# One store for the last group's output, and larger, earlier loads in the first third, in a tree-masked attention kernel

## The chip, the core and the metric

The kernel runs on one core of one Trainium2 chip. The time is the device time of one execution in microseconds, the median of several runs. A profile is one execution taken by the hardware profiler; its span is the time from the first instruction to the last, and the profiled execution's own time is a little longer than its span.

## The reference

Eight batches of twelve heads make 96 heads. Each has 512 queries and keys of 64 numbers. The mask lets a query see itself and its ancestors in a binary heap:

```python
mask = np.zeros((seq, seq))
for i in range(seq):
    mask[i, i] = 1
    parent = i
    while parent > 0:
        parent = (parent - 1) // 2
        mask[i, parent] = 1
scores = np.einsum('bhqd,bhkd->bhqk', Q, K) / np.sqrt(dim) + (1 - mask) * (-1e9)
weights = np.exp(scores - scores.max(-1, keepdims=True))
weights = weights / (weights.sum(-1, keepdims=True) + 1e-10)
return np.einsum('bhqk,bhkd->bhqd', weights, V).astype(np.float32)
```

Q, K, V and the output are each 96 x 512 x 64 floats, 12.58 MB.

## The kernel before, in words

The work is cut into 48 pairs of heads (loop index `i`) and into 12 groups of eight heads, or four pairs, each (index `g`). "q24" below means the load of Q for the heads from 24 on; v, k and q name V, K and Q.

**Loads.** `load_v`, `load_k` and `load_q` (line 189) issue one DMA each from GpSimd's queue. The DMA casts from float32 in DRAM to bf16 in SBUF, so an eight-head load reads 1 MB and writes 512 KB; a four-head load is half of that. There are four buffers of eight heads for each of V, K and Q. Which loads are issued after which pair is a table written out by hand, `loads_at` (line 447): the dictionary `early` up to pair 12, and one load per pair from a formula after that.

**One pair.** TensorE transposes K and Q of the pair into PSUM (line 250), VectorE copies them out (line 276), TensorE makes scores for two key tiles (lines 287 to 316), ScalarE takes the exponentials (lines 298 and 321), TensorE multiplies by V (line 347), and VectorE normalises (reciprocal, line 376, and multiply, line 377) into an output tile `of` of the group. Transposes run two pairs ahead: in turn `i` of the main loop (line 497) the order is scores of pair `i`, values and normalisation of pair `i-1`, transposes and copy of pair `i+2`, then `spread(i)` and `pool(i)`.

**Spreading V.** The values of a group have to be copied into a second layout `vt` (line 209). `spread(i)` (line 425) divides these copies among VectorE, GpSimd and, early on, ScalarE. From pair 6 on the first of GpSimd's copies in a turn waits for the VectorE copy of the same turn (`after`, line 390), so that the two alternate. These are GpSimd's "waiting copies".

**GpSimd's queue.** It holds, in program order, the spread copies of a turn and after them, from `pool(i)` (line 473), the loads and the stores of the turn. An instruction that waits holds everything behind it. The DMAs that it issues use eight completion semaphores in turn, so each DMA also waits for the landing of the one eight before it.

**Stores.** `store` (line 384) writes output heads to DRAM, from GpSimd's queue as well; an eight-head store is 1 MB, since the output is float32. `pool(i)` begins to store at pair 33, one group per turn, and takes any group that is complete. After turn 46 the first four heads of group 11, the last, are stored on their own (line 511). In turn 48 the loop in `pool` reaches group 11 too and stores all eight heads. After the loop, heads 4 and 5 and heads 6 and 7 of the group are stored once more (lines 512 and 513). Each of these stores writes DRAM rows that an earlier one wrote, or overlaps it, and the program makes it wait for the landing of that earlier store.

Of the kernel before, what the change touches and what calls it, by code (L numbers as in the profile page):

```python
# [98 lines left out]
def kernel(  # L99
# [15 lines left out]
    NG = NH // GB  # L115
# [68 lines left out]
    def load(kept, pool, name, src, h0, n):  # L184

        g = h0 // GB
        if g not in kept:
            kept[g] = pool.tile([P, GB, 4, D], bf16, name=name)
        nc.gpsimd.dma_start(  # L189
            out=kept[g][:, h0 % GB:h0 % GB + n, :, :].rearrange("p h t d -> p h (t d)"),  # L190
            in_=src[:, h0:h0 + n, :],
        )
# [191 lines left out]
    def store(g, h0=0, n=GB):  # L384
        nc.gpsimd.dma_start(  # L385
            out=Or[:, GB * g + h0:GB * g + h0 + n, :],
            in_=ofs[g][:, h0:h0 + n, :, :].rearrange("p h t d -> p h (t d)"),
        )
# [58 lines left out]
    def loads_at(i):  # L447

        k4 = lambda h: [(load_k, h, 4), (load_q, h, 4)]
        start = [(load_v, 0, 4), (load_k, 2, 2), (load_q, 2, 2)] + k4(4) + [(load_v, 4, 4)]  # L450
        start += k4(8) + [(load_v, 8, 4)] + k4(12)
        early = {
            -1: start, 1: [(load_v, 12, 4), (load_v, 16)],
            2: [(load_k, 16, 4), (load_q, 16, 4), (load_k, 20, 4)],
            3: [(load_q, 20, 4), (load_v, 24), (load_k, 24, 4)], 5: [(load_q, 24, 4)],
            6: [(load_k, 28, 4)], 7: [(load_q, 28, 4), (load_v, 32)],
            8: [(load_k, 32), (load_q, 32)], 9: [(load_v, 40)], 10: [(load_k, 40)],
            11: [(load_q, 40), (load_v, 48)], 12: [(load_k, 48), (load_q, 48)],
        }
        if i in early:  # L460
            return early[i]
        g, j = i // 4 + 3, i % 4
        if i < 13:
            return []
        if j == 0:
            return [(load_q, GB * g)] if g < NG else []
        if j < 3 and g + 1 < NG:
            return [((load_v, load_k)[j - 1], GB * (g + 1))]
        return []

    stored = []

    def pool(i):
        for f, *args in loads_at(i):
            f(*args)
        if i >= 33:
            for g in range(len(stored), (i - 4) // 4 + 1):
                if len(stored) < i - 32:
                    stored.append(g)
                    store(g)  # L480

    AHEAD = {1: (2, 3), 2: (), 3: (4, 5)}

    pool(-1)
    fill(0, 8)
    first_pair()
# [10 lines left out]
    for i in range(1, NP + 1):  # L497
        if i < NP:
            scores1(i)
            scores2(i)  # L500
        if i >= 2:
            values(i - 1)
            norm(i - 1, ((0, 1), (1, 2)) if i == NP else ((0, 2),))
        for n in AHEAD.get(i, (i + 2,)):
            if n < NP:
                transpose(n)
                evac(n)
        spread(i)
        pool(i)
        if i == NP - 2:  # L510
            store(NG - 1, 0, 4)
# [32 lines left out]
```

## Time and profile before

| what | us |
|---|---|
| median of 3 runs | 148.3 (147.78 to 149.77) |
| the profiled execution's own time | 149.07 |
| its span | 147.3 |
| last normalisation starts (VectorE, line 377) | 130.27, 0.42 long |
| last store issued (GpSimd, line 385) | 143.3 |

| engine | busy us | share of the span |
|---|---|---|
| TensorE, matmuls | 114.8 | 78% |
| VectorE | 103.0 | 70% |
| GpSimd | 96.2 | 65% |
| ScalarE | 92.6 | 63% |

DMA is not in this table. Its share and its rate stand in the page's part 2, in 40 slices of the span, 3.68 us each. The rate counts the bytes written: while loads run it is about 198 GB/s, with twice as many bytes read, and while stores run about 400 GB/s. A timeline line gives the start, the length, the engine, the source line, the operation, the tiles, and in brackets how long the engine idled before it and what ended that. The DMA view gives, for the issues in a stretch of time, the time from issue to landing. The chain is followed back from the last instruction to what released it.

### The profile page before, as it was taken

How to read it: one execution, taken by the hardware profiler on the slowest of the kernel's cores; microseconds unless marked ns; L12 is line 12 of the kernel's file. 1: busy time of each engine (PE TensorE's matmuls, PEld its weight loads, DVE VectorE, ACT ScalarE, POOL GpSimd, SP SyncE). 2: the span in 40 equal slices, each digit the busy share in tenths (PEclk: the TensorE clock that was granted, in tenths of full speed). 3: DMA queues.
4: the chain of work that ended last, by engine and by line, in shares of the span. 5: the costliest groups of instructions: out<-in, count | busy, mean ns of one | idle time of the engine just before them, and what ended most of it. 6: DMA issues, size and time to landing. Idle time of an engine off the chain costs nothing. (4 is left out here: it accounts for less than half of the span.)

```text
span 147.3 us, 5481 instructions
## 1 busy us (share of the span) xinstructions
PE 114.8 (78%) x2413; PEld 80.7 (55%) x2413; DVE 103.0 (70%) x215; ACT 92.6 (63%) x110; POOL 96.2 (65%) x134
## 2 busy tenths in 40 slices
PE   6787769998989599999997998998979889910000
PEld 2345547666767377777675775765757566610000
DVE  2586767897999559999796988889887795530000
ACT  4187927999888357887775776777748585800000
POOL 7965996059879974869967588589786873200221
PEclk9999968999999869999999999999999999995555
DMA  4999999998799999999999999999999999995243
GB/s 125 223 194 199 193 197 197 197 188 106 98 191 198 199 197 199 197 198 202 194 199 197 198 201 194 199 197 206 341 399 402 404 397 405 399 394 215 110 176 142
DMA packets 41418, 33.39 MB, mean 227 GB/s; under 512 B 1034, under 2 KB 38026, under 8 KB 41394
## 3 DMA queue, kind: packets, MB, share of 16 engines
q0 software_dynamic: 40656, 32.25, 117.7%
q1 hardware_dynamic: 466, 0.53, 1.1%
q8 instruction: 19, 0.31, 0.8%
q10 hardware_dynamic: 272, 0.26, 0.6%
q14 instruction: 5, 0.04, 0.1%
HBM read 38.01 MB, written 13.63 MB: 351 GB/s over the span
## 5 line engine op out<-in xcount | busy, mean ns | idle before, releaser
L298 ACT ACTIVATE e<-s 128x1024 bf16<-128x1024 f32 x48 | 49.1, 1023 | 32.5 <-PE s L292 32.1
L209 POOL COPY vt<-vst 32x512 bf16<-32x512 bf16 (+2 forms) x69 | 46.5, 674 | 28.6 <-DVE vt L209 22.7
L347 PE MATMUL ob<-vt,e 128*128 128x65 bf16 (+1 forms) x940 | 38.4, 198 | 2.2 <-DVE of L377 0.7
L321 ACT ACTIVATE e<-s 128x768 bf16<-128x768 f32 x48 | 38.7, 806 | 0.3 <-PE s L316 0.3
L347 PEld LDWEIGHTS <-e 128*128 128x128 bf16 (+1 forms) x960 | 31.0, 103 | 10.4 <-issue 2.1
L276 DVE COPY kq<-kqp 128x1024 bf16<-128x1024 bf16 x48 | 32.8, 683 | 5.3 <-PE kqp L250 5.1
L377 DVE TENSOR_TENSOR of<-ob,rec 128x512 f32<-128x512 f32 x47 | 32.5, 692 | 1.6
L209 DVE COPY vt<-vst 32x1024 bf16<-32x1024 bf16 (+2 forms) x60 | 28.4, 473 | 1.6
L385 POOL DMA_DIRECT2D out_dram<-of x15 | 12.8, 857 | 18.1 <-issue 9.4
L250 PE MATMUL kqp<-ptile,kst 128*64 128x128 bf16 x384 | 20.0, 225 | 4.2 <-DVE kq L276 2.0
L250 PE MATMUL kqp<-ptile,qst 128*64 128x128 bf16 x384 | 19.9, 225 | 2.8 <-DMA qst<-in_Q_dram 1.8
L287 PE MATMUL s<-ctile 40*128 40x512 bf16 x96 | 19.2, 395 | 1.2 <-ACT e L298 1.0
L316 PEld LDWEIGHTS <-kq 64*128 64x128 bf16 x384 | 14.7, 95 | 9.5 <-issue 2.4
L292 PE MATMUL s<-kq 64*128 64x512 bf16 x96 | 18.9, 388 | 1.2 <-issue 0.7
L376 DVE RECIPROCAL rec<-ob 128x8 f32<-128x8 f32 x47 | 9.7, 207 | 14.4 <-PE ob L347 12.6
L316 PE MATMUL s<-kq 64*128 64x64 bf16 (+1 forms) x384 | 18.2, 211 | 1.2 <-issue 1.2
L310 PE MATMUL s<-ctile 40*128 40x480 bf16 x96 | 18.0, 370 | 0.5
L250 PEld LDWEIGHTS <-kst 128*64 128x64 bf16 x384 | 13.5, 113 | 5.9 <-issue 5.0
L250 PEld LDWEIGHTS <-qst 128*64 128x64 bf16 x384 | 14.4, 114 | 3.1 <-DMA qst<-in_Q_dram 2.0
L189 POOL DMA_DIRECT2D kst<-in_K_dram x16 | 13.3, 834 | 0.0
L189 POOL DMA_DIRECT2D qst<-in_Q_dram x16 | 13.3, 832 | 0.0
L189 POOL DMA_DIRECT2D vst<-in_V_dram x14 | 12.2, 874 | 0.9 <-POOLq L528 0.8
(22 smaller groups left out, 38.5 us busy)
## 6 DMA issues: line engine op xcount, KB each, us to landing
out_dram<-of POOLq DMA_DIRECT2D x12, 1024.0 KB, 13.0
vst<-in_V_dram POOLq DMA_DIRECT2D x10, 512.0 KB, 13.5
kst<-in_K_dram POOLq DMA_DIRECT2D x8, 512.0 KB, 14.7
qst<-in_Q_dram POOLq DMA_DIRECT2D x8, 512.0 KB, 13.5
kst<-in_K_dram POOLq DMA_DIRECT2D x7, 256.0 KB, 9.7
qst<-in_Q_dram POOLq DMA_DIRECT2D x7, 256.0 KB, 10.2
vst<-in_V_dram POOLq DMA_DIRECT2D x4, 256.0 KB, 7.4
out_dram<-of POOLq DMA_DIRECT2D x1, 512.0 KB, 9.6
```

The source lines that it names most:

```text
L189: nc.gpsimd.dma_start(out=kept[g][:, h0 % GB:h0 % GB + n, :, :].rearrange("p h t d -> p h (t d)"), in_=src[:, h0:h0 + n, :],)
L209: return (eng.copy if eng is nc.scalar else eng.tensor_copy)(out=out, in_=in_)
L250: nc.tensor.transpose(out=dst, in_=st[2 * i // GB][:, 2 * i % GB + a, t, :], identity=perm)
L276: nc.vector.tensor_copy(out=kq[:, :, :, :].rearrange("p k (x y) c -> p k x y c", y=2), in_=src)
L287: nc.tensor.matmul(out=sp[:, a, :], lhsT=k1code[64 * a:64 * a + BITS, :], rhs=q1code[64 * a:64 * a + BITS, :], start=True, stop=False,)
L292: nc.tensor.matmul(out=sp[:, a, :], lhsT=keys(i, a, TOP), rhs=qTs[i][64 * a:64 * a + 64, :, :].rearrange("p t c -> p (t c)"), start=False, ...
L298: nc.scalar.activation(out=et[:, :, :, :].rearrange("p a t c -> p (a t c)"), in_=sp[:, :, :].rearrange("p a c -> p (a c)"), func=AF.Exp, s ...
L310: nc.tensor.matmul(out=flat[:, a, 32:512], lhsT=k2code[64 * a:64 * a + BITS, :], rhs=q2code[64 * a:64 * a + BITS, 32:512], start=True, sto ...
L316: nc.tensor.matmul(out=flat[:, a, lo:hi], lhsT=keys(i, a, TILE2[t]), rhs=qTs[i][64 * a:64 * a + 64, :, :].rearrange("p t c -> p (t c)")[:, ...
L321: nc.scalar.activation(out=e2s[i % NE][:, :, :, 32:128].rearrange("p a t c -> p (a t) c"), in_=sp[:, :, :, 32:128].rearrange("p a t c -> p ...
L347: nc.tensor.matmul(out=ob[lo:hi, a, 65 * t:65 * t + 65], lhsT=e[:, a, PLACE[t], lo:hi], rhs=vt[:, 2 * i % GB + a, tile_v, 0:D + 1], **flags,)
L377: nc.vector.tensor_tensor(out=ofs[g][:, 2 * r + a0:2 * r + a1, :, :], in0=o4[:, :, :, 0:D], in1=rec[:, :, :, :].to_broadcast([P, a1 - a0, ...
```

## The change

Two things change. In `pool`, the loop over groups stops before the last one, so group 11 is stored only in the three parts: heads 0 to 3 after turn 46, heads 4 and 5, and heads 6 and 7. In `early`, the K and Q loads of heads 16 to 31 are made by eight heads in place of four, and the loads of heads 16 to 39 are issued in turns 1, 2, 3 and 5, where they were issued in turns 1 to 8. The loads of heads 40 and above keep their turns.

```diff
         early = {
-            -1: start, 1: [(load_v, 12, 4), (load_v, 16)],
-            2: [(load_k, 16, 4), (load_q, 16, 4), (load_k, 20, 4)],
-            3: [(load_q, 20, 4), (load_v, 24), (load_k, 24, 4)], 5: [(load_q, 24, 4)],
-            6: [(load_k, 28, 4)], 7: [(load_q, 28, 4), (load_v, 32)],
-            8: [(load_k, 32), (load_q, 32)], 9: [(load_v, 40)], 10: [(load_k, 40)],
+            -1: start, 1: [(load_v, 12, 4), (load_v, 16), (load_k, 16)], 2: [(load_q, 16)],
+            3: [(load_v, 24), (load_k, 24)],
+            5: [(load_q, 24), (load_v, 32), (load_k, 32), (load_q, 32)],
+            9: [(load_v, 40)], 10: [(load_k, 40)],
             11: [(load_q, 40), (load_v, 48)], 12: [(load_k, 48), (load_q, 48)],
         }
...
         if i >= 33:
-            for g in range(len(stored), (i - 4) // 4 + 1):
+            for g in range(len(stored), min((i - 4) // 4, NG - 2) + 1):
                 if len(stored) < i - 32:
                     stored.append(g)
                     store(g)
```

## The prediction

> **What bounds the kernel now.** I began at the end, with the chain of work that ended last (start, length, what; us):
>
> ```profile
> 127.30 0.76 DMA out_dram<-of
> 128.06 9.40 issue
> 137.46 0.01 POOLq L385
> 137.47 4.86 DMA out_dram<-of
> 142.33 0.28 issue
> 142.62 0.71 POOL out_dram L385
> 143.32 0.71 POOLq L539
> ```
>
> The stores of the last group follow one another. Four heads are issued at 127.30, all eight at 137.47, landing 4.86 later, and the first quarter at 142.62. VectorE's timeline says that nothing else is left to do by then; this is its last line:
>
> ```profile
> 130.27 0.42 DVE L377 TENSOR_TENSOR of<-kqp,rec 128x256 f32<-128x256 f32 x1
> ```
>
> Computing is over at 130.69, so 16.6 us of the span of 147.31 are stores. Next I read DMA issues and their time to landing, and the bytes on the page:
>
> ```profile
> HBM read 38.01 MB, written 13.63 MB: 351 GB/s over the span
> out_dram<-of POOLq DMA_DIRECT2D x12, 1024.0 KB, 13.0
> out_dram<-of POOLq DMA_DIRECT2D x1, 512.0 KB, 9.6
> out_dram<-of POOLq DMA_DIRECT2D x2, 256.0 KB, 2.5
> ```
>
> The output is 12.58 MB, and 1.05 MB more is written. The half store, issued at 127.30, lands 9.6 later, at 136.9; only then does the eight-head store go out, which overwrites the same rows. The "issue" of 9.40 is this wait.
>
> Then the page's slices, for what stands ahead of the end:
>
> ```profile
> DMA  4999999998799999999999999999999999995243
> GB/s 125 223 194 199 193 197 197 197 188 106 98 191 198 199 197 199 197 198 202 194 199 197 198 201 194 199 197 206 341 399 402 404 397 405 399 394 215 110 176 142
> ```
>
> DMA is the bound for most of the run: 9 in every slice from the second to the 36th, except two. Those two, 33 to 40 us, move 106 and 98 GB/s where the neighbours move 198. GpSimd's timeline shows why:
>
> ```profile
> 22.08 1.70 POOL L209 COPY vt<-vst 32x256 bf16<-32x256 bf16 x4
> 23.73 0.74 POOL L189 DMA_DIRECT2D qst<-in_Q_dram  x1
> 30.79 1.25 POOL L209 COPY vt<-vst 32x512 bf16<-32x512 bf16 x2 [6.31 <-DVE vt L209]
> 31.99 0.74 POOL L189 DMA_DIRECT2D kst<-in_K_dram  x1
> ...
> 35.38 0.89 POOL L189 DMA_DIRECT2D vst<-in_V_dram  x1
> ```
>
> After q24 at 23.73 GpSimd sits 6.31 us before a copy, with the next loads behind it. The queue runs dry; TensorE pays later, waiting 1.84 for q32:
>
> ```profile
> 49.58 0.41 PE L250 MATMUL kqp<-ptile,qst 128*64 128x128 bf16 x8 [1.84 <-DMA qst<-in_Q_dram]
> ```
>
> **The end, step by step.** The change removes one 1 MB store, the wait ahead of it and the wait behind it. The quarter stores then follow their normalisations. Heads 4 and 5 are ready at 129.05 (line 377 at 128.36, 0.69 long), heads 6 and 7 at 130.69. They write rows that nothing else writes, so their only late condition is data. Two ends for their landing:
> - By data alone: 130.75 plus 2.54, what the last quarter took (143.31 to 145.85), is 133.3.
> - By the queue: landings come in the order of issue. The half store lands at 136.94; half a megabyte at 400 GB/s behind it takes 1.3, giving 138.2. If each quarter took its lone 2.5 after the half store, it would be 5.0, giving 141.9; that needs them to follow singly, and 1 MB stores in this queue land 2.6 apart, against 4.86 for the lone one.
>
> The queue is later, so it decides: 138.2. From the last landing to the span's end it takes 147.31 - 145.85 = 1.46 now, which stays. Span 139.7: the store part alone gains **7.6**. It is uncovered, since nothing else runs.
>
> **The gap, step by step.** In the new order of GpSimd's queue k16 and q16 (eight heads) go out in turns 1 and 2, v24 and k24 in turn 3, and q24, v32, k32 and q32 right after the copy group of 22.08. At 0.74 to 0.90 per issue that group of four takes 23.73 to about 27.2, ahead of the copy of 30.79, which loses nothing. Four loads fewer save GpSimd 4 x (2 x 0.75 - 0.88) = 2.5 us, worth nothing while it waits.
>
> What the queue gains: in the stretch 31 to 43 us it moved 132 GB/s against 198, which is 12 x (1 - 132/198) = 4.0 us of lost transfer. By landings it is 3.6: q24 landed at 34.8 (23.73 + 11.1); k28, q28 and v32 at 1.33, 1.33 and 2.65 (512 KB at 198 GB/s is 2.65) would land v32 at 40.2, and it landed at 43.8 (35.38 + 8.4). How much reaches the end? DMA must not run dry later. The tightest issue is the last load, q88, at 95.49: it lands 11.4 later, while v32 on an emptied queue took 8.4. So 3.0 are to spare; beyond that the shift is lost unless computing is earlier too. The stores have more: 11.6 and 13.6 for the first and the eleventh, against 4.86 for a lone one. Between 3.0 and 3.6 I take **3.3**. The bounds are 4.0 and nothing; below nothing only by a computing delay, priced next.
>
> The Trainium skill (page "DMA: Bandwidth & Descriptors", section "Anatomy of one DMA — SWDGE (gpsimd) path") gives each DMA a fixed 2.0 us besides bytes over 436 GB/s. The lone 1 MB store's 4.86 stands near its 4.4. Charged per load, four loads fewer would be worth 8 us and the forecast would be near 129; but four-head and eight-head loads alike kept 198 GB/s here while the queue was full, so I give the merging nothing.
>
> **The wait that is added.** q16 now brings eight heads. Before, four heads landed at 26.8 (16.45 + 10.3), and TensorE used them at 28.10. Now v16, k16 and q16 follow v12 (14.10 + 7.4 = 21.5) at 2.65 each, so q16 lands at 29.5: TensorE stalls 1.4 in the transposes of pair 8, and behind them, in its order, are the scores of pair 7, the exponentials, everything. The wait at 49.58 goes in exchange: q32 lands after v24, k24, q24, v32, k32 and itself, 29.5 + 6 x 2.65 = 45.4, ahead of 47.7, when TensorE began to wait. That wait cost more than 1.84. Normalisations of pairs 14 and 15 came 4.33 and 2.97 apart, against 2.3 around them, together 2.7, because the granted clock was 0.72 in 49 to 55 us and 1.00 before. If the new stall draws the same clock it costs 2.7 as well. So computing ends between 1.3 earlier and the same; I take 0.7 earlier, 130.0. It does not set the end (133.3 - 0.7 = 132.6 by data against the queue), but becomes late next if DMA does better.
>
> **The sum.** Half store 136.94 - 3.3 = 133.6; quarters + 1.3 = 134.9; tail + 1.46 = 136.4 of span, a gain of 7.6 + 3.3 = 10.9. Outside the span lie 149.07 - 147.31 = 1.76, so the profiled execution would be 138.1. The median of the runs shown is 0.77 lower than the profiled execution: 148.3 - 10.9 = **137.4**.
>
> **Rivals** (on the scale of the median).
> 1. The stores alone help. The queue is filled at 27 us but runs dry later, because the loads' issues are paced by the pairs. For it: pairs come about 2.3 apart and DMA needs 2.0 per pair (3 x 2.65 / 4), so it catches up with the issues. Against it: the spare of 3.0 at q88 is nearly the whole shift. 148.3 - 7.6 = 140.7.
> 2. DMA does better and computing sets the end. In 132 to 137 us it moves 195 GB/s, half its rate, with a share of 0.50: its engines end one after another. Together they would move those 5 x 195 = 975 KB in 2.4, so the half store would land at 134.4, less 3.3 is 131.1, and the quarters at 132.4. Then data decide, at 133.3 - 0.7 to 133.3 - 1.3: span 133.5 to 134.1, time 134.5 to 135.1. For it: idle stretches in which the engines catch up with one another; against it: nothing in the change evens them out.
> 3. The late q16 costs much more than the removed wait saves: 1.4 + 2.7 = 4.1 with nothing given back. Data decide at 133.3 + 4.1, span 138.9, time 139.9.
> 4. Slower than before: the four loads in turn 5 hold GpSimd until earlier ones land. Then its copies of group 2, which TensorE needs from pair 8 on, move from 30.79 to 45.4, 14.6 later, and with them every later pair: 133.3 + 14.6 + 1.46 = 149.4 of span, 150.3. It decides only if more loads are on their way than GpSimd can issue. Against it: at 27.2 seven eight-head loads would be on their way; the load issued at 52.69 took 18.6 to land, seven times 2.65, so there were as many then, and its issue took 0.87. The eight semaphores don't hold it either: q32 waits for v16, landed by 24.2.
>
> That the change doesn't do what it says is excluded for the stores: the second store of group 11 is gone from the queue, and the quarters wait for no store of this group.
>
> **How the numbers follow.** Forecast 0.58; rival 1 0.20; rival 2 0.13; rival 3 0.06; rival 4 0.03. The range takes in rivals 1 to 3 and the ends of the gap's cost (4.0 to nothing): 134.5 to 141.2; the quarters singly, 137.4 + 3.7 = 141.1, are just in. A measurement of this kernel can tell about 2% from no change (its runs spread 1.3%), that is 145.3 to 151.3. All cases but the fourth lie under 145: faster 0.96. Rival 4 lies within 2% at 150.3, and above it if the copies slip further: same 0.02, slower 0.02.
>
> **What would show it.** Stores of 1024 KB: eleven, not twelve; written 12.58 MB; the chain without the 9.40; the quarters issued near 128.4 and 130 and landing within 2 of the half store; no slice near 100 GB/s at 33 to 40 us; GpSimd's four issues end by 27.5; a TensorE wait for q16 near 28, none for q32 near 48. The forecast is wrong if DMA goes idle between 80 and 110 us, if computing ends after 132, or if the quarters land one by one.

## The result, and the profile after

| | before | after |
|---|---|---|
| median, us | 149.04 (147.78 to 150.61, 4 runs) | 138.38 (137.67 to 139.34, 4 runs) |
| the profiled execution's own time | 149.07 | 137.91 |
| its span | 147.3 | 136.2 |
| last normalisation ends (VectorE) | 130.69 | 130.77 |
| last store lands | 145.85 | 134.66 |

The ratio is 0.9315, with a 95% interval of 0.9202 to 0.9428. The forecast was 137.4, and a span of 136.4. A ratio compares the fast runs of both kernels and leaves out those over 1.5% above a kernel's fastest; medians here are of all runs.

The chain of work that ended last (start, length, what) now ends like this; these lines answer to those with the wait of 9.40:

```profile
122.14 0.88 POOL out_dram L385
123.02 4.35 issue
127.39 0.76 POOL out_dram L385
128.15 1.27 issue
129.44 0.71 POOL out_dram L385
130.16 0.89 issue
131.05 0.74 POOLq L538
```

No store waits for another any more. The half store goes out at 127.39, and the quarters at 129.44 and 131.07, each as soon as its normalisation is done. The last line of VectorE's timeline is where it was:

```profile
130.35 0.42 DVE L377 TENSOR_TENSOR of<-kqp,rec 128x256 f32<-128x256 f32 x1
```

So computing ended at the same time as before, and the whole gain of 11.1 us of span lies in the stores and in DMA. The page's bytes, DMA shares and rates in 40 slices, here of 3.4 us:

```profile
DMA  4999999999999999999999999999999999999971
GB/s 115 226 189 195 197 196 198 199 197 199 202 194 200 197 200 197 198 197 198 197 199 200 195 199 197 198 198 198 202 306 406 401 402 394 402 390 398 375 303 48
...
HBM read 38.01 MB, written 12.58 MB: 372 GB/s over the span
```

The two slices near 100 GB/s are gone, and nothing is written twice. GpSimd's timeline in the first third shows why the queue stays full: four loads go out in a row, and only then comes the copy that waits.

```profile
22.89 0.98 POOL L189 DMA_DIRECT2D qst<-in_Q_dram  x1
23.86 0.88 POOL L189 DMA_DIRECT2D vst<-in_V_dram  x1
24.72 0.89 POOL L189 DMA_DIRECT2D kst<-in_K_dram  x1
25.58 0.90 POOL L189 DMA_DIRECT2D qst<-in_Q_dram  x1
31.32 1.25 POOL L209 COPY vt<-vst 32x512 bf16<-32x512 bf16 x2 [4.83 <-DVE vt L209]
```

What sets the end now is read from the issues. The DMA view, for the half store and the two quarters in turn:

```profile
out_dram<-of POOLq DMA_DIRECT2D x1, 512.0 KB, 6.0
out_dram<-of POOLq DMA_DIRECT2D x1, 256.0 KB, 4.6
out_dram<-of POOLq DMA_DIRECT2D x1, 256.0 KB, 3.6
```

So the half store (127.39) lands 6.0 later, the first quarter (129.44) 4.6 later and the last (131.07) 3.6 later: 133.4, 134.0, 134.7. They land 0.6 apart, which is 256 KB at 400 GB/s, though they were issued 1.6 apart; a lone quarter took 2.5 before. They stand in the queue. The experiments had to show whether that reading is right, and how the gain divides.

### The profile page after: what moved, and what is told of

The parts are those of the page before. It is cut to its first block, busy times and chain, and to the rows that moved or that the text cites. A ratio compares the mean times of both kernels' runs of the same rounds, so it can differ in the third digit from the quotient of the medians.

```text
span 136.2 us, 5474 instructions
## 1 busy us (share of the span) xinstructions
PE 116.5 (86%) x2413; PEld 81.0 (60%) x2413; DVE 102.8 (75%) x215; ACT 92.5 (68%) x110; POOL 93.1 (68%) x129
## 4 chain that ended last, share of the span: by engine, by line
PE 47%; DMA 15%; POOL 14%; issue 12%; DVE 5%; ACT 3%; POOLq 1%; ACTq 0%
PE ob L347 16%; PE kqp L250 10%; DMA qst<-in_Q_dram 9%; PE s L287 7%; DMA vst<-in_V_dram 5%; PE s L316 5%; PE s L292 5%; PE s L310 5%; POOL vt L209 5%; POOL vst L189 3%; POOL qst L189 2%; POOL kst L189 2%; DVE vt L209 2%; POOL out_dram L385 2%; DVE of L377 2%
## 5 line engine op out<-in xcount | busy, mean ns | idle before, releaser
L385 POOL DMA_DIRECT2D out_dram<-of x14 | 12.0, 854 | 6.6 <-DVE of L377 6.6
L310 PEld LDWEIGHTS <-ctile 40*128 40x128 bf16 x96 | 7.3, 97 | 8.7 <-issue 2.5
L189 POOL DMA_DIRECT2D qst<-in_Q_dram x14 | 12.2, 872 | 0.0
```

Source lines behind the costliest of these rows:

```text
L189: nc.gpsimd.dma_start(out=kept[g][:, h0 % GB:h0 % GB + n, :, :].rearrange("p h t d -> p h (t d)"), in_=src[:, h0:h0 + n, :],)
L310: nc.tensor.matmul(out=flat[:, a, 32:512], lhsT=k2code[64 * a:64 * a + BITS, :], rhs=q2code[64 * a:64 * a + BITS, 32:512], start=True, sto ...
```

## The experiments

My theory: the two parts add. The second store of group 11 cost 7.6, its waits more than its bytes; the gap at 31 to 43 us cost about 3.4; the queue, not computing, sets the end. Against it stood: the earlier loads don't reach the end; computing sets the end; the size of the loads counts, not their turn.

### The stores alone

```diff
-            for g in range(len(stored), (i - 4) // 4 + 1):
+            for g in range(len(stored), min((i - 4) // 4, NG - 2) + 1):
```

> Only the stores are changed: group 11 is stored in three parts, and the loads stay as before. Theory: the two parts of the change add. The half store still lands near 136.9, the quarters near 138.2, the span is near 139.7, 7.6 under the 147.3 of before and 3.5 over the 136.2 of the full change; the two slices near 100 GB/s at 33 to 40 us stay. Rival A (the end belongs to computing, and the earlier loads don't reach it): the span is within 1 of the full change, 135 to 137. Rival B (what the second store cost is partly paid again by the queue, as quarters that land one by one): 141 or more.

Measured: median 141.11, ratio 0.9448 (0.9346 to 0.9550), profiled span 138.6, last landing 137.2. That is 8.0 under the before of the same runs by the medians, against 7.6 expected. The gap is still there:

```profile
GB/s 104 250 191 197 196 197 199 194 200 178 109 168 198 204 195 202 195 198 198 198 197 199 202 194 199 197 198 198 198 295 392 407 397 400 404 398 407 398 252 32
```

It was smaller in this execution. Of the stretch 31 to 43 us, the first line is from the kernel before, the second from this one; the last number is GB/s:

```profile
31.00:43.00 12.00, 10.96 (x240) 7.67 (x234) 10.71 (x22) 11.02 (x14) 10.02 (x15) 1.00 1.03 132
31.00:43.00 12.00, 10.73 (x250) 7.76 (x246) 10.68 (x22) 10.24 (x12) 10.15 (x15) 1.00 1.20 158
```

The half store landed at 135.9 in place of 136.9. The last line of VectorE's timeline is the telling one:

```profile
127.32 0.42 DVE L377 TENSOR_TENSOR of<-kqp,rec 128x256 f32<-128x256 f32 x1
```

Computing ended at 127.7, 3.0 earlier than in the full change, and yet the last landing came 2.5 later. The quarters were issued at 126.40 and 128.04 and took 10.2 and 9.2 to land. Here the end clearly belongs to the queue. Rival A falls, and so does rival B: the half store and the quarters landed 0.6 to 0.7 apart, and the four spans were 138.4 to 139.7.

### The loads alone

The diff is the `early` table of the change, with the loop over groups left as it was.

> Only the loads are changed; group 11 is still stored twice. Theory: the whole queue runs 3.5 earlier, the half store lands near 133.4, and behind it the chain of before follows unchanged (0.5 wait, 4.9 for the 1 MB store, then the quarters): span 147.3 - 3.5 = 143.8. Rival A (earlier loads don't reach the end): 146.5 to 147.5. Rival C (earlier loads give more than the gap, since the stores start from an earlier last load): under 142.5.

Measured: median 145.6, ratio 0.9771 (0.9686 to 0.9856), span 143.5, which is 3.8 less than before; 3.5 was expected. The chain keeps its old form and begins earlier:

```profile
125.73 0.77 DMA out_dram<-of
126.50 7.09 issue
133.58 0.01 POOLq L385
133.60 4.85 DMA out_dram<-of
```

The half store lands at 133.1 (7.3 after its issue), 3.9 earlier than before. Rivals A and C fall: the four spans were 143.3 to 144.2. By the medians the two parts alone gain 8.0 and 3.5, together 11.5; the whole change gained 10.7, and the intervals are about 1.5 wide on either side. They add within what these runs can tell.

### The early turns, by four heads

```diff
-            -1: start, 1: [(load_v, 12, 4), (load_v, 16), (load_k, 16)], 2: [(load_q, 16)],
-            3: [(load_v, 24), (load_k, 24)],
-            5: [(load_q, 24), (load_v, 32), (load_k, 32), (load_q, 32)],
+            -1: start, 1: [(load_v, 12, 4), (load_v, 16), (load_k, 16, 4)],
+            2: [(load_q, 16, 4), (load_k, 20, 4), (load_q, 20, 4)],
+            3: [(load_v, 24), (load_k, 24, 4), (load_k, 28, 4)],
+            5: [(load_q, 24, 4), (load_q, 28, 4), (load_v, 32), (load_k, 32), (load_q, 32)],
```

> The full change, but K and Q of heads 16 to 31 are loaded by four heads, in the early turns. It tells the turn from the size. Theory: the turn counts. GpSimd still gets its loads out before its first waiting copy near 31 (the last of them waits for the landing of the load eight before, near 29), DMA keeps 198 GB/s without a gap, and the span is that of the full change, 136.2 within 1; the wait for q16 near 29 goes. Rival D (the size counts, 2.0 fixed per DMA): four DMAs more cost up to 8, span 138 to 144. Rival E (eight loads under way hold GpSimd): its first waiting copy slips past 32 and pairs from 8 on with it, span 137 to 139.

Measured: median 137.99, ratio 0.9247 (0.9192 to 0.9302), span 135.9. GpSimd was held by earlier landings, but not long enough to matter:

```profile
28.47 0.88 POOL L189 DMA_DIRECT2D kst<-in_K_dram  x1 [0.44 <-PE kqp L250]
29.79 0.88 POOL L189 DMA_DIRECT2D qst<-in_Q_dram  x1 [0.44 <-issue]
30.94 1.25 POOL L209 COPY vt<-vst 32x512 bf16<-32x512 bf16 x2 [0.28 <-DVE vt L209]
```

The DMAs eight issues before these two had landed at 27.9 and 29.3, just ahead of each issue: that is the wait for one of the eight completion semaphores. Four DMAs more cost nothing that these runs show, and TensorE waits for no load after the start. The turn counts; rivals D and E fall. Computing ended at 127.8, 3.0 earlier than in the full change, and the last landing moved from 134.7 to 134.5: a second sign that the queue decides.

### Eight heads, but the loads of heads 32 to 39 late

```diff
-            5: [(load_q, 24), (load_v, 32), (load_k, 32), (load_q, 32)],
+            5: [(load_q, 24)], 7: [(load_v, 32)], 8: [(load_k, 32), (load_q, 32)],
```

> The full change, but the eight-head loads of heads 32 to 39 stay in turns 7 and 8, behind GpSimd's first waiting copies. Theory: the turn counts. The queue holds work until q24 lands near 37.4, v32 goes out near 34.7 and lands 6.0 to 8.4 later, 40.9 to 43.1, against 40.1 in the full change: the span is 0.8 to 3.0 longer, 137 to 139.2. Rival D (the size counts): within 0.5 of the full change.

Measured: ratio 0.9337 (0.9246 to 0.9428), span 138.6 in the profile and 136.8 and 137.4 in two other executions. GpSimd's timeline:

```profile
22.68 0.98 POOL L189 DMA_DIRECT2D qst<-in_Q_dram  x1
31.38 1.25 POOL L209 COPY vt<-vst 32x512 bf16<-32x512 bf16 x2 [7.72 <-DVE vt L209]
35.55 1.26 POOL L209 COPY vt<-vst 32x512 bf16<-32x512 bf16 x2 [2.91 <-DVE vt L209]
36.76 0.88 POOL L189 DMA_DIRECT2D vst<-in_V_dram  x1
```

v32 landed 5.7 after its issue, at 42.5, against 40.1 in the full change, and two slices fell to 71 and 140 GB/s. By the profile it is 2.4 of span longer, within what was expected. The whole-run ratio does not separate it from the full change, and 136.8 and 137.4 lie within the spans of the full change's four runs (135.9 to 137.6). What the run shows is that the gap comes back with the late turns, not what it costs.

### Without the half store

```diff
-        if i == NP - 2:
-            store(NG - 1, 0, 4)
```

Heads 88 to 91 are left out of the output.

> The full change without the half store: heads 0 to 3 of group 11 (heads 88 to 91 of the output) are left out, half a megabyte less in the queue just ahead of the quarters. Theory (the queue decides the end): 1.3 less, a span of 134.9, and the last quarter lands about 2.5 after its issue. Rival 2 (computing and the last quarter's own latency decide): the last quarter is issued and lands as before, span 136.2 within 0.5.

Measured: ratio 0.9406 (0.9245 to 0.9567), span 137.3. Two other executions had 136.8 and 136.5, against 135.9 to 137.6 in the full change: the 1.3 that the theory had asked for is not seen. In the profiled execution computing ended at 133.1. TensorE waited 2.24 for q16, against 0.47 in the full change's profile, and later, in the last pair, for no releaser that the profile shows:

```profile
29.65 0.41 PE L250 MATMUL kqp<-ptile,qst 128*64 128x128 bf16 x8 [2.24 <-DMA qst<-in_Q_dram]
...
130.84 1.01 PE L347 MATMUL kqp<-vt,e 128*128 128x65 bf16 x20 [1.65 <-issue]
```

The last quarter went out at 133.37 and landed 2.5 later, which is what a lone one takes. So in this execution computing set the end, as rival 2 of the prediction had it, though not by a better DMA: the last eight-head store landed at 133.4, 1.5 later than in the full change. In the full change's own profile the last quarter took 3.6, so there computing lies 1.1 behind the queue. The run says nothing on the half store, and it was repeated on the kernel with four-head loads:

> The early loads by four heads, without the half store (heads 88 to 91 of the output are left out). In the same test on the full change computing ended late, at 133.0, after a 2.24 wait for q16 and a 1.64 wait of TensorE for its instructions, and so hid what the half store is worth. With four-head loads the wait for q16 is gone and computing ended at 127.8. Theory (the queue decides): half a megabyte less is 1.3 less than with that store, span 135.9 - 1.3 = 134.6. Rival 2 (computing decides): 135.9 within 0.4.

Measured: ratio 0.9394 (0.9292 to 0.9496), span 135.0, against 135.9 with the half store: 0.9 less, where 1.3 was expected. GpSimd's last two issues:

```profile
126.38 0.71 POOL L385 DMA_DIRECT2D out_dram<-of  x1 [6.40 <-DVE of L377]
128.02 0.72 POOL L385 DMA_DIRECT2D out_dram<-of  x1 [0.93 <-DVE of L377]
```

They took 6.5 and 5.6 to land. From the landing of group 10 to the last landing it is 1.3 (132.3 to 133.6); with the half store it was 2.6 (131.9 to 134.5). Inside the trace the half store is worth its 1.3; the rest is that group 10 landed 0.35 later in this execution. The ratios of the two kernels don't tell 0.9 us.

### A second megabyte that waits for nothing

```diff
+        if i == NP - 3:
+            store(0)
         if i == NP - 2:
             store(NG - 1, 0, 4)
```

> The full change with group 0 stored a second time, after turn 45, just ahead of the half store. These rows were landed long before, so the second megabyte waits for nothing: it is the double store of before without its waits. Theory (the queue decides): 1.05 MB at 400 GB/s is 2.6, span 138.8. Rival 2 (computing decides): the extra store hides partly and the span grows by 1 or less. If 2.6 is measured, then of what the second store of the last group cost in the kernel before (8.0 by the comparison with the stores changed alone), 2.6 were its bytes and about 5 the two waits for landings.

Measured: median 140.52, ratio 0.9486 (0.9350 to 0.9623), span 137.9, which is 1.7 more than the full change's, between the theory and rival 2. The run times cannot tell 2.6 from 1: the ratio of the full change was 0.9315 in one set of runs and 0.9392 in another. The trace tells more. The extra store landed 2.55 after the one ahead of it (131.64, 134.19), the last quarter 2.1 later than in the full change (136.76 against 134.66). The last issues:

```profile
128.14 0.76 POOL L385 DMA_DIRECT2D out_dram<-of  x1 [3.75 <-DVE of L377]
130.51 0.71 POOL L385 DMA_DIRECT2D out_dram<-of  x1 [1.61 <-DVE of L377]
131.84 0.72 POOL L385 DMA_DIRECT2D out_dram<-of  x1 [0.63 <-DVE of L377]
```

The last quarter landed 4.9 after its issue at 131.84. The queue carries the megabyte to the end nearly whole, 2.1 of the 2.6. Hence a second megabyte that waits for nothing costs 2.1 to 2.6. In its old place the second store put 8.9 us between the landings of the half store and of the last quarter, against 1.3 with the stores alone: 7.6 more, of which some 5.0 to 5.5 were the two waits. This is a difference between single executions.

### The last stores from SyncE

```diff
-    def store(g, h0=0, n=GB):
-        nc.gpsimd.dma_start(
+    def store(g, h0=0, n=GB, eng=None):
+        (eng or nc.gpsimd).dma_start(
...
-    store(NG - 1, 4, 2)
-    store(NG - 1, 6, 2)
+    store(NG - 1, 4, 2, nc.sync)
+    store(NG - 1, 6, 2, nc.sync)
```

> The full change, with the two quarter stores issued from SyncE in place of GpSimd. Theory: the bytes of each DMA engine stay what they are, and the engines that end last set the end, so the span is 136.2 within 0.7. Rival F (the quarters stand behind the half store only because they share its queue, and on a queue of their own land about 2 after their issue near 131): span 134.5 to 135.3.

Measured: ratio 0.9287 (0.9136 to 0.9439), span 135.9, against 136.2. SyncE's queue in the timeline, and its issues in the DMA view:

```profile
128.41 2.02 SPq L385 DMA_DIRECT2D out_dram<-of  x2
```

```profile
out_dram<-of SPq DMA_DIRECT2D x2, 256.0 KB, 5.5
```

On a queue of their own the quarters still took 5 and 6 us to land, beside the half store's 7.3. Rival F falls: leaving GpSimd's queue did not let them land early. The DMA view from 126 to 134 us shows both queues at work, GpSimd's first (packets, MB, share of 16 engines):

```profile
q0 software_dynamic: 557, 2.08, 66.5%
q1 hardware_dynamic: 505, 0.49, 17.3%
```

The half store landed at 133.9 and the quarters at 134.4 and 135.0, so they seem to share the DMA engines with it. SyncE's packets are 1 KB and GpSimd's 4 KB; whether larger packets would have landed sooner is not tested. The span is no longer, although the last landing came 0.35 later than in the full change: from there to the end it took 0.90, against 1.49.

The same on the four-head loads, with the half store from SyncE as well, was the candidate for the fastest version. It ran twice, the second time beside the full change:

> The early loads by four heads, with all three stores of the last group issued from SyncE: the candidate for the fastest version. Theory: with the early loads by four heads computing ended 3 earlier (127.8) and the last landing moved only from 134.7 to 134.5, so the queue decides and SyncE changes little: span 135.9 within 0.7. Rival F: the last group's stores overtake what waits in GpSimd's queue and land by 131.5, but the stores ahead of them still have to land, so the span is no less than the landing of the half store's predecessor, 131.9, plus 1.5: 133.4 to 134.5.

> The early loads by four heads with the last group's stores from SyncE, once more beside the full change. Expected: about 137.3, 0.5 to 1.5 less than the full change, and a smaller spread, since the wait for q16 does not occur.

> The full change once more, beside the candidate for the fastest version on the same chip. Expected: about 138.4, with the wait of TensorE for q16 near 29 anywhere between 0.5 and 2.2 as in the runs so far, and spans between 136 and 139.

Measured: first 137.32, ratio 0.9296 (0.9203 to 0.9389), span 135.1; then 138.44, ratio 0.9400 (0.9331 to 0.9468), span 136.8. The full change beside it: ratio 0.9392 (0.9297 to 0.9486). The expected 0.5 to 1.5 of advantage was not seen. The first span is 0.8 under the 135.9 that the theory had, but the half store landed at 132.9, just behind the store ahead of it (132.7): rival F falls here too. The full change's profile of that set (span 137.8) had no wait for q16 at all: its first normalisation came at 12.5, against 11.8 in the first profile, and q16 landed only 0.3 later. In it computing ended at 132.9, and the last quarter, issued at 133.18, landed 3.1 later, 0.6 more than a lone one takes: queue and computing lie close together there. The four-head loads take away the wait for q16, but these runs don't show a version that beats the change.

## Why the prediction was right, point by point

- **The stores alone, 7.6**: measured 8.0 by the medians and 8.7 by the profiles, of which 1.0 belongs to a smaller gap in that execution. The division was right: 0.53 of wait, 4.86, and 3.52 to the last landing, less the 1.3 of the quarters, are 7.6.
- **The quarters behind the half store, 1.3 and not 5.0**: 133.4 to 134.7, 1.2. They pass as a stream.
- **The gap, 3.3 at the end**: the half store landed 3.5 earlier than before in the full change and 3.9 earlier in the loads alone. That it came so near 3.3 is partly luck. At q88 the shift was 4.6, over my bound of 4.0 (0.4 of it stood already at v16, whose turn had not changed). Issued at 93.72, q88 landed at 102.2. It took 8.5, about the 8.4 at which I had put the limit, but its issue had come 1.8 earlier as well, because the pairs were earlier by then. Among the stores 1.1 was lost again: the sixth landed 4.9 earlier than before, the seventh 3.7. Why is not known. Rival 1 is out.
- **Merging the loads is worth nothing**: right. The Trainium skill (page "DMA: Bandwidth & Descriptors", section "Anatomy of one DMA — SWDGE (gpsimd) path") charges about 2.0 us for each DMA; by an estimate from that figure four more would cost 8. Here, with four loads more in the early turns the ratio was 0.9247, against 0.9315. In a queue that did not empty the charge does not appear; the lone 1 MB store of before took 4.86, 2.3 more than the 2.6 between landings in a full queue, so a lone transfer shows a charge of that size.
- **The wait for q16, 1.4**: right in the middle and wrong as a single number. It was 0.47 in the full change's profile and 1.42, 2.11, 2.24, 1.69 and 0.93 in the other profiles with that load where it showed. The granted clock in 28 to 36 us was 1.00 after waits of 0.47, 0.93 and 1.42, 0.79 after 1.69 and 2.24, and 0.57 after 2.11: lower after the three longest, though not in their order. One line of the full change and one of the kernel with late loads:

```profile
29.27 0.41 PE L250 MATMUL kqp<-ptile,qst 128*64 128x128 bf16 x8 [0.47 <-DMA qst<-in_Q_dram]
```

```profile
29.50 0.64 PE L250 MATMUL kqp<-ptile,qst 128*64 128x128 bf16 x8 [2.11 <-DMA qst<-in_Q_dram]
```

- **The end of computing, 130.0**: the term that was off. It was 130.77, and the quarters went out at 129.44 and 131.07, 1.0 later than the 128.4 and 130 that I had given. The wait for q32 did go, and the pairs were 1.8 earlier up to pair 38 (106.56 against 108.34 for its normalisation). Then TensorE sat idle:

```profile
108.17 0.41 PE L250 MATMUL kqp<-ptile,kst 128*64 128x128 bf16 x7 [1.77 <-issue]
```

  The clock was granted at 0.79 in 106 to 114 us, and the lead was lost. Over all the profiles computing ended between 126.8 (four-head loads with the stores from SyncE) and 133.1 (without the half store). With the early loads by four heads it was 126.8 to 129.4 in four profiles, with the eight-head loads 129.1 to 133.1 in seven, and with the old loads 127.7 and 130.7. So the larger loads may cost computing time that the queue hides; no run shows it apart from the scatter. The prediction called itself wrong if computing ended after 132: in the second profile of the full change it did (132.9), with a span of 137.8. A step that takes this end from one profile to half a microsecond claims too much. It did little harm, since the queue was later; without the half store it wasn't.
- **Rival 2** was put at 0.13. In one profile, with half a megabyte less in the queue, computing set the end, but DMA had not done better. **Rivals 3 and 4** did not occur: the four issues ended at 26.5, as forecast (27.2), and held nothing.
- **The sum**: 136.4 of span forecast, 136.2 measured; 138.1 forecast for the profiled execution, 137.91 measured; 137.4 forecast, 138.38 the median. The miss lies in the last step: it took off 0.77 because the median of before lay that far under its profiled execution, and after the change the median lies 0.47 over it. That is scatter between executions: the full change's own medians in two sets of runs were 138.38 and 139.36. So the 0.2 in the span is closer than one profile can promise.

## What to carry to other kernels

Where DMA is the bound, look first for a queue that runs dry: a slice of the profile with half the usual rate, and at its start an issuing engine that waits in an instruction with the next loads behind it. Bytes are worth their time at the queue's rate and no more, but a store that overwrites rows of a store under way costs that landing too, and at the end of this kernel nothing hid it. When a transfer-bound kernel gets faster, the time of computing is the next bound: ask how much it varies from run to run, not only when it ended once.

## What I had not expected of the hardware

- TensorE's instructions come by DMA, as far as the traces tell. The page has a queue of kind "instruction" with 19 packets and 0.31 MB, 16 KB each. TensorE's idle times put down to "issue" fall on instructions 2744, 3255, 3766, 4021, 4276 and 4532 in the kernel before, counting matmuls and weight loads: 255 to 256 apart, or twice that. All 4826 are 18.9 times 256. In the full change a packet of that queue ended at 106.7, and TensorE went on at 108.2. Over the profiles such a wait was 0.3 to 2.0 long. The longest stood at 4021, where stores had taken the place of loads; 1.8 to 2.0 of it came only with the eight-head early loads, in five of their seven profiles, and 0.9 to 1.2 elsewhere. That the waits are for these packets is not tested by an experiment.
- The DMA engines of one transfer end far apart. In the kernel before, the queue moved 195 GB/s on average from 132 to 137 us, half its rate, until the last engine's part of the half store had landed. The 16 parts of that store landed over 4.4 us, those of the first loads over 0.8.
- An eight-head load issued on an emptying queue took 8.4 to land in the kernel before and 5.7 in the run with late loads. I don't know why.
